# Hybrid encoder step in FP32: the down projection's token operands split piece by piece in the gate/up units, weight tiles kept through both feed-forward stages, the last unit multiplied by quarters

## The chip, the cores and the metric

The kernel runs on one core of one Trainium2 chip. The metric is the device time of one execution in microseconds (us). The kernel before took 2544.37 us, the median of three runs (2538.43, 2544.37 and 2545.0). Engines are called as the profile calls them: PE is TensorE (matmuls), PEld its weight loads, DVE is VectorE, ACT ScalarE, POOL GpSimd, SP SyncE, whose queue issues nearly all DMAs.

## The reference, cut to what matters

One layer of an encoder: attention, an output projection with a residual, then a feed-forward part with a residual, and a last norm. All inputs and outputs are float32. There are 576 new tokens (512 prompt frames and 64 frames of a running stream; 16 meta tokens take part in the attention alone). The change touches only the end:

```python
x = x + mix @ lp['w_out']
h = rmsnorm(x, lp['norm_ffn_g'])
x = x + (jax.nn.silu(h @ lp['ffn_w_gate']) * (h @ lp['ffn_w_up'])) @ lp['ffn_w_down']
...
y_prompt = rmsnorm(xp[:, N_META:], final_norm_g)
y_sample = rmsnorm(xs, final_norm_g)
```

The model width is 2048 and the hidden width of the feed-forward part 5632.

## The kernel before, in words

*Precision.* Every float32 operand of a matmul is split into a high part in the matmul's format (fp32r), written by a copy on ACT, and a low part, the operand less the high part, written by a subtraction on DVE. Three matmuls stand for one: weights high times tokens high, high times low, and low times high. `split` does this for weights, `builder` and `operand` for tokens. Instructions of ACT, DVE and SP go through one wrapper, so that they all have line L125 in the profile; tiles tell them apart: `wh`, `wl` are the weights' parts, `bh`, `bl` the tokens', `ws` sums of weight blocks, `raw` the loaded weights, `m` the PSUM banks, `c` the gate or up result of a unit, `y` the output rows, `ot` the finished output tiles.

*Winograd form.* The three feed-forward matrices are multiplied in a 2 x 2 form with seven products instead of eight (`winograd`, from line 1069). Of the weights, some products take a block as it is loaded (1, 2, 4) and some take a sum of blocks (5, 6, 3, 7): POOL makes two of these sums (line 1096), DVE the other two. Of the tokens there are likewise seven operands: three plain quarters and four sums of quarters. `CHAIN` and `WIDE` give the order of the products and which of them add into the same PSUM bank; `take` moves a bank into the result after each product, and then `step` is called, a hook through which the caller places other work. Matmuls of lines 1127 and 1131 are those of the products (1131 the low weights).

*Gate and up.* The loop over 22 units `u` (line 1281) computes 256 columns of gate, then of up. One product has 8 weight blocks, so 24 matmuls of 128x288; one half of a unit (gate or up) has seven. Weights come in two `raw` blocks of 1 MB for each half, from three buffers (one in the pool `rw`, two in `fr`). After "up", POOL multiplies gate by up in two halves (line 1316) and makes the four sums of quarters for the down projection (1322 to 1325); the result goes to the DRAM tensor `actspill`, the sums to `sumspill`.

*Down projection.* The 22 units are taken in blocks of 4, 4, 4, 4, 4 and 2. For each block a loop over eight pairs of output column tiles (`d`) multiplies the block's weights, by `winograd` with 4 weight blocks (12 matmuls a product), and adds each product into `y`. The operands of the next block are loaded by `builder` from `actspill` and `sumspill` (144 KB each, 28 for a block), and split one step at a time behind the products. There are eight operand slots, four for the current block and four for the next. The operands of block 0 are loaded and split in the last "up" half, from its third product on. The last block of two units is done plainly (`plain_rows`, `mm3` at line 205), token half by token half, and `finish` transposes each half (line 1395), scales it and stores it through `ot`, four buffers in turn.

*Pools.* Tiles live in pools that are opened and closed like a stack. Between the stages `fb` (results and sums of gate/up), `rw` and `fw` (weight parts) are closed, and `yy` (the output rows) and `yp` (weight parts of the down projection) are opened in the same space.

*Order.* PE runs in the order in which a scheduler at build time puts its matmuls; so do the other engines, except for instructions marked by `pin` or by `ordered`, which keep the order of the program text. Each engine then works through its list in order, and so does SP's queue with its DMAs.

Of the kernel before, what the change touches and what calls it, by code (L numbers as in the profile page):

```python
# [2 lines left out]

# [128 lines left out]
def encoder_step(  # L132
# [196 lines left out]
    sumspill = dp.tile([FC // 2, P, 4, QH], F32, name="sumspill")  # L329
    mspill = dp.tile([KC, P, TQ], F32, name="mspill")  # L330
# [674 lines left out]
    rb2 = rw.tile([P, TQ], F32, name="rb2")  # L1005
    sq2 = rw.tile([P, TQ], F32, name="sq2")
# [13 lines left out]

    def operand(m, p, src):
        hi = bc.tile([P, QH], F32R, name=f"bh{p}_{m}")
        lo = bc.tile([P, QH], F32R, name=f"bl{p}_{m}")
        pin(S.activation(hi, src, AF.Copy))
        pin(V.tensor_tensor(lo, src, f32(hi), op=ALU.subtract))
        operands[m, p] = (hi, lo)
# [41 lines left out]

    def winograd(wpool, spool, raws, slots, take, banks=None, engine=V, step=lambda: None, stag=("ws", 3),
# [117 lines left out]
    close_ma()  # L1187
    fb, close_fb = pool("fb", "right")


    def stile():
        return fr.tile([P, QH], F32, name="s", tag="s", bufs=4)

    def combined(c11, c12, c21, c22, chain):
# [15 lines left out]
        def take(p, banks):  # L1210
            if p == 1:
                s[1] = stile()
                S.activation(s[1], banks[1], AF.Copy)
            elif p == 6:
                s[2] = stile()
# [13 lines left out]
    def builder(m0, count, plain, ahead, by_product=False):  # L1229

        srcs = {}
        for m in range(m0, m0 + count):
            quarter = [actspill[2 * m + f, :, c] for f in range(2) for c in (slice(0, QH), slice(QH, TQ))]
            if plain:
                for p, src in zip((1, 2, 4, 5), quarter):
                    srcs[m, p] = src
            else:
                for p, src in zip(ORDER, (quarter[0], quarter[2], sumspill[m, :, 2], sumspill[m, :, 0],
                                          sumspill[m, :, 1], quarter[3], sumspill[m, :, 3])):
                    srcs[m, p] = src  # L1240
        order = [p for p, _ in CHAIN]
        todo = sorted(srcs, key=lambda mp: order.index(mp[1])) if by_product else list(srcs)

        def fetch(n):
            for m, p in todo[n:n + 1]:
                hi = bc.tile([P, QH], F32R, name=f"bh{p}_{m % 8}")
                lo = bc.tile([P, QH], F32R, name=f"bl{p}_{m % 8}")
                load(f32(lo), srcs[m, p])
                operands[m % 8, p] = (hi, lo)

        for n in range(ahead):
            fetch(n)
        for n, (m, p) in enumerate(todo):
            fetch(n + ahead)
            hi, lo = operands[m % 8, p]
            pin(S.activation(hi, f32(lo), AF.Copy))
            yield
            pin(V.tensor_tensor(lo, f32(lo), f32(hi), op=ALU.subtract))
            yield
# [17 lines left out]

    turn = 0
    norm = token_norm()
    start = builder(0, blocks[0], False, 4, True)  # L1280
    for u in range(FC // 2):
        out = {}
        for which, wsrc in (("g", w_gate), ("u", w_up)):
# [9 lines left out]
            take = combined(*quarters(c[:, 0, :], c[:, 1, :]), chain)  # L1293
            done = [0]

            def step():
                if u == 0 and which == "u":
                    next(norm, None)
                if u == FC // 2 - 1 and which == "u":
                    done[0] += 1  # L1300
                    if done[0] > 2:
                        for _ in range(2 * blocks[0]):
                            next(start, None)

            if first:
                winograd(fw, fb, raws, range(4, 8), take, banks0, step=step)
            else:
                winograd(fw, fb, raws, range(8), take, step=step, chain=chain)
# [4 lines left out]
        if u == 0:  # L1313
            gated(g)
        for f in range(2):
            G.tensor_tensor(w[:, f, :], w[:, f, :], g[:, f, :], op=ALU.mult)
            if u < FC // 2 - 1:
                store(actspill[2 * u + f], w[:, f, :])
        if u < FC // 2 - blocks[-1]:
# [6 lines left out]
            store(sumspill[u], t)  # L1326
    for _ in start:
        pass
    for f in range(2):
# [7 lines left out]
    y = []  # L1337

    def plain_rows(m0, n, d, hs, slots, done):
# [3 lines left out]
        for g in range(0, n, 2):  # L1343
            for f in range(2):
                wh = yp.tile([P, 4, P], F32R, name="wh", tag="wh", bufs=2)
                wl = yp.tile([P, 4, P], F32R, name="wl", tag="wl", bufs=2)
# [6 lines left out]
        for f in range(2):  # L1353
            for h in hs:
                c = y[2 * d + f][:, h * QH:(h + 1) * QH]
# [3 lines left out]
    def down_rows(m0, n, d, slots, step):  # L1359
        raws = [load_raw(fr, w_down, m0 * 256, 2 * n, d * 256, 2)]  # L1360
        y11, y12, y21, y22 = quarters(y[2 * d], y[2 * d + 1])
# [6 lines left out]
        winograd(yp, yp, raws, slots, take, step=step, chain=CHAIN)  # L1368
# [3 lines left out]

    def squares(i, h):
        c = y[i][:, h * QH:(h + 1) * QH]
        if i == 0:
            sqs[h] = stile()
            G.tensor_tensor(sqs[h], c, c, op=ALU.mult)
        else:
            t = stile()
# [4 lines left out]
    def finish(h, ahead):  # L1384
# [6 lines left out]
        def turned(q, j):  # L1391
            o, n = tok[h][j]
            ps = pmt()
            for k in range(4):
                PE.transpose(ps[0:n, k * P:(k + 1) * P], y[q * 4 + k][:, o:o + n], ident)
# [7 lines left out]
        vc = yp.tile([P, 3], F32, name=f"vc{h}")  # L1403
        rc = yp.tile([P, 3], F32, name=f"rc{h}")
# [24 lines left out]
    for bi, n in enumerate(blocks):  # L1429
        slots = [(first + k) % 8 for k in range(n)]  # L1430
        if bi + 1 < len(blocks):
            build = builder(first + n, blocks[bi + 1], bi + 2 == len(blocks), 4)
# [4 lines left out]
            for d in range(KC // 2):  # L1437
                if bi == 0:
                    for i in (2 * d, 2 * d + 1):
                        y.append(yy.tile([P, TQ], F32, name=f"y{i}"))  # L1440
                        load(y[i], x2spill[i])
# [3 lines left out]
        else:  # L1445
            before = iter(())
# [10 lines left out]
    close_yp()  # L1457
    close_fr()
    close_yy()
    close_bc()  # L1460
# [74 lines left out]
```

## Time and profile before

| | |
|---|---|
| median of 3 runs | 2544.37 us (2538.43 to 2545.0) |
| the profiled execution, its own time | 2546.21 us |
| its span, first to last instruction | 2544.4 us |
| mean granted TensorE clock | 0.989 |
| PE busy | 2449.5 us, 96% |
| DVE, ACT, POOL busy | 1801.7, 1107.4, 744.8 us |
| gate and up | about 1020 to 1972 us |
| down projection with its end | about 1972 to 2544 us |

The span is the time on which all rows of the trace lie; the execution's own time is 1.8 us longer. Busy shares are averages over stages with different limits, so the stages are looked at one by one. A matmul's busy time is modelled and overlaps the next one's, so the count of matmuls in a stretch says more than the busy share. "A <- B" in a row of waits says that A stood idle until B was done.

### The profile page before, as it was taken

Reading aid. Unit: us, or ns where it says so; the run is one execution under the profiler, and the core shown is the slowest. Engines: PE = TensorE matmul, PEld = TensorE weight load, DVE = VectorE, ACT = ScalarE, POOL = GpSimd, SP = SyncE. Lnnn points to the kernel's source line nnn. Section 1 sums busy time; section 2 is a strip of 40 time slices with the busy share of each in tenths; the row PEclk is TensorE's granted clock in tenths of the full one; section 3 lists DMA queues with packets and bytes.
Section 4 is the critical chain, followed back from the end, with each engine's and each line's share of the span. In section 5 each row is a group of like instructions: output and inputs, shape, how many; then the busy total and the mean of one; then the engine's idle time right before and its main releaser. Section 6 shows DMA issues by size and latency. Waiting matters only on the chain. (4 is left out here: it accounts for less than half of the span.)

```text
span 2544.4 us, 44870 instructions
## 1 busy us (share of the span) xinstructions
PE 2449.5 (96%) x17847; PEld 2390.0 (94%) x17847; DVE 1801.7 (71%) x2826; ACT 1107.4 (44%) x2008; POOL 744.8 (29%) x621
## 2 busy tenths in 40 slices
PE   7999999989999999999999999999999899999997
PEld 6999999988999888999999999999999899999997
DVE  5555555556555567877777777777777899999975
ACT  5343333334434344444444444444445444444445
POOL 0000000010000165644545445454543222222236
PEclk9999999999999999999999999999999999999999
DMA  6533232334232453333333333333335642542334
GB/s 197 156 87 87 80 85 75 82 94 143 88 92 80 152 154 117 123 133 119 124 101 130 124 123 133 115 119 108 128 128 162 210 150 83 164 150 83 114 97 149
DMA packets 330116, 307.73 MB, mean 121 GB/s; under 512 B 24708, under 2 KB 298507, under 8 KB 329907
## 3 DMA queue, kind: packets, MB, share of 16 engines
q1 hardware_dynamic: 329346, 302.80, 37.9%
q8 instruction: 140, 2.29, 0.4%
q0 software_dynamic: 560, 2.06, 0.2%
q14 instruction: 70, 0.57, 0.1%
HBM read 250.82 MB, written 56.68 MB: 121 GB/s over the span
## 5 line engine op out<-in xcount | busy, mean ns | idle before, releaser
L1127 PE MATMUL m<-bh,wh 128*128 128x288 f32 x3584 | 968.9, 296 | 10.8 <-ACT wh L125 10.7
L1127 PE MATMUL m<-bl,wh 128*128 128x288 f32 x3584 | 968.1, 295 | 0.0
L1127 PEld LDWEIGHTS m<-bh,wh 128*128 128x128 f32 x3584 | 674.5, 188 | 11.8 <-ACT wh L125 11.7
L1127 PEld LDWEIGHTS m<-bl,wh 128*128 128x128 f32 x3584 | 678.0, 189 | 0.1
L1131 PE MATMUL m<-bh,wl 128*128 128x288 f32 x3584 | 585.9, 299 | 18.4 <-DVE wl L125 15.4
L1131 PEld LDWEIGHTS m<-bh,wl 128*128 128x128 f32 x3584 | 512.8, 189 | 31.9 <-DVE wl L125 31.4
L1096 POOL TENSOR_TENSOR ws<-raw 128x512 f32<-128x512 f32 x256 | 344.0, 1352 | 600.5 <-DVE wl L125 321.7
L125 ACT ACTIVATE wh<-ws 128x512 fp32r<-128x512 f32 (+1 forms) x340 | 288.8, 849 | 449.4 <-PE m L1127 300.8
L125 DVE TENSOR_TENSOR wl<-ws,wh 128x512 fp32r<-128x512 f32 (+1 forms) x340 | 379.5, 1116 | 115.1 <-ACT wh L125 114.5
L125 DVE TENSOR_TENSOR wl<-raw,wh 128x512 fp32r<-128x512 f32 x416 | 403.5, 984 | 25.9 <-ACT wh L125 16.1
L125 ACT ACTIVATE wh<-raw 128x512 fp32r<-128x512 f32 x416 | 249.8, 626 | 310.3 <-PE m L1127 277.3
L108 PE MATMUL ps<-xh,wh 128*128 128x296 f32 x960 | 222.1, 313 | 4.9 <-ACT xh L125 3.7
L108 PE MATMUL ps<-xl,wh 128*128 128x296 f32 x960 | 212.0, 302 | 0.8 <-DVE xl L125 0.8
L108 PE MATMUL ps<-xh,wl 128*128 128x296 f32 x960 | 211.9, 302 | 0.9 <-DVE wl L125 0.9
L108 PEld LDWEIGHTS ps<-xh,wh 128*128 128x128 f32 x960 | 157.8, 192 | 9.0 <-ACT xh L125 3.8
L125 DVE TENSOR_TENSOR y<-y,m 128x288 f32<-128x288 f32 x312 | 140.0, 449 | 28.7 <-PE m L1131 17.9
L108 PEld LDWEIGHTS ps<-xh,wl 128*128 128x128 f32 x960 | 158.3, 191 | 1.6 <-DVE wl L125 1.6
L108 PEld LDWEIGHTS ps<-xl,wh 128*128 128x128 f32 x960 | 158.7, 192 | 1.1 <-DVE xl L125 1.1
L125 DVE TENSOR_TENSOR ws<-ws,raw 128x512 f32<-128x512 f32 x128 | 92.4, 722 | 84.3 <-POOL ws L1096 77.6
L125 DVE TENSOR_TENSOR wl<-wr,wh 128x1024 fp32r<-128x1024 f32 (+1 forms) x110 | 119.6, 1087 | 44.5 <-ACT wh L125 43.0
L125 ACT ACTIVATE wh<-wr 128x1024 fp32r<-128x1024 f32 (+1 forms) x110 | 101.7, 929 | 73.1 <-PE ps L108 51.7
L1274 POOL TENSOR_TENSOR c<-c,rb 128x576 f32<-128x576 f32 x44 | 73.2, 1666 | 165.5 <-ACT c L125 162.9
(359 smaller groups left out, 3352.7 us busy)
## 6 DMA issues: line engine op xcount, KB each, us to landing
raw<-in_ffn_w_gate SPq DMA_DIRECT2D x44, 1024.0 KB, 7.2
raw<-in_ffn_w_up SPq DMA_DIRECT2D x44, 1024.0 KB, 5.9
raw<-in_ffn_w_down SPq DMA_DIRECT2D x40, 1024.0 KB, 5.7
wr<-in_w_in SPq DMA_DIRECT2D x60, 512.0 KB, 4.0
actspill<-c SPq DMA_DIRECT2D x44, 288.0 KB, 2.1
sumspill<-c SPq DMA_DIRECT2D x20, 576.0 KB, 2.8
bl<-sumspill SPq DMA_DIRECT2D x80, 144.0 KB, 3.6
bl<-actspill SPq DMA_DIRECT2D x68, 144.0 KB, 3.9
```

The source lines that it names most:

```text
L108: self.tc.keep_in_program_order(self.pe.matmul(out, lhsT, rhs, start=start, stop=stop))
L125: ins = issue(*args, **kwargs)
L1096: engine.tensor_tensor(w[:, k:k + m, :], pick(xs), pick(ys), op=op)
L1127: PE.matmul(banks[p], wh[:, k, :], x, start=first and new and k == 0 and x is hi, stop=False, skip_group_check=not new)
L1131: PE.matmul(banks[p], wl[:, k, :], hi, start=False, stop=last and k == n - 1, skip_group_check=not new)
L1274: G.tensor_tensor(g[:, f, :], g[:, f, :], rb2, op=ALU.mult)
```

## The change

1. **Token operands split in the gate/up loop.** Units 2 to 19 no longer store their result and sums for the down projection as they are. In the next unit, `parts` splits the seven operands one at a time (ACT high part, DVE low part, into a tile of two parts) and stores each with both parts in a new DRAM tensor `partspill`. In the down projection `fetcher` loads the two parts (288 KB) straight into the operand slot. Units 0 and 1 keep the old way, and so do the last two units, which the plain block uses.
2. **Block 0.** `starter` loads its operands after each product of the last "up" half, from the first product on, and splits only those of units 0 and 1, two products later. SP's order is pinned there. The weights for its first two column pairs are fetched ahead by `fetch_raw`, the first before that half, the second after it.
3. **Weight tiles.** `fw` (weight parts) and a new pool `fs` (sums of weight blocks) stay open through both stages. `weight_tiles` gives the down projection, which needs tiles of four blocks, the two halves of a tile of eight.
4. **Output rows.** `y0` and `y1` take the space of the two norm rows, `y2` to `y4` that of the weight buffer in `rw`; the others come from `yy`, which is opened after the first column pair.
5. **Last unit.** Its multiplication of gate by up is done in quarters on POOL, each when its quarter is complete.
6. **Last block.** Sums of squares and output tiles lie in free operand slots (30 of them) instead of tiles of four buffers.

The number and shapes of the matmuls are the same. The diff, cut to its core:

```diff
+    def weight_tiles(wpool, n):
+        if n == 8 or not spare:
+            both = [wpool.tile([P, 8, P], F32R, name=x, tag=x, bufs=2) for x in ("wh", "wl")]
+            if n == 8:
+                return both
+            spare.append([w[:, 4:8, :] for w in both])
+            return [w[:, 0:4, :] for w in both]
+        return spare.pop()
...
-            wh = wpool.tile([P, n, P], F32R, name="wh", tag="wh", bufs=2)
-            wl = wpool.tile([P, n, P], F32R, name="wl", tag="wl", bufs=2)
+            wh, wl = weight_tiles(wpool, n)
...
+    def fetch_parts(m, p):
+        load(f32(operand_tile(m % 8, p)), partspill[m, :, PIECE[p]])
...
+    def starter():
...
+        todo = [p for p, _ in CHAIN]
+        for i in range(len(todo) + 2):
+            if i < len(todo):
+                for m in range(blocks[0]):
+                    if m < WHOLE:
+                        fetch_whole(m, todo[i], whole(m, todo[i]))
+                    else:
+                        fetch_parts(m, todo[i])
+            if i > 1:
+                for m in range(WHOLE):
+                    split_in_place(m, todo[i - 2])
+            yield
...
+    def parts(u, srcs):
+        for p in ORDER:
+            b = fb.tile([P, 2, QH], F32R, name="parts", tag="parts", bufs=2)
+            S.activation(b[:, 0, :], srcs[PIECE[p]], AF.Copy)
+            V.tensor_tensor(b[:, 1, :], srcs[PIECE[p]], f32(b[:, 0, :]), op=ALU.subtract)
+            store(partspill[u, :, PIECE[p]], f32(b))
+            yield
...
+            ending = u == FC // 2 - 1 and which == "u"
+            if ending:
+                Q.ordered = True
+                fetch_raw(0, blocks[0], 0)
...
+                def take(p, banks):
+                    combine(p, banks)
+                    if p in (2, 7, 3, 4):
+                        q = {2: 0, 3: 1, 4: 2, 7: 3}[p]
+                        G.tensor_tensor(w[q], w[q], g[q], op=ALU.mult)
...
+                done[0] += 1
+                if which == "u" or done[0] > 3:
+                    next(pieces, None)
+                if ending:
+                    next(start)
...
+            if u < WHOLE:
+                store(sumspill[u], t)
+            else:
+                pieces = parts(u, [b11, b12, b21, b22] + [t[:, i, :] for i in range(4)])
     for _ in start:
         pass
+    fetch_raw(0, blocks[0], 1)
...
+    accumulator(0, rw.tile([P, TQ], F32, name="y0", tag="rows", bufs=2))
+    accumulator(1, rw.tile([P, TQ], F32, name="y1", tag="rows", bufs=2))
+    y234 = rw.tile([P, 8 * 256], F32, name="y234", tag="raw", bufs=1)
...
-    close_fb()
-    close_rw()
-    yy, close_yy = pool("yy", "right")
-    close_fw()
-    yp, close_yp = pool("yp")
...
-            build = builder(first + n, blocks[bi + 1], bi + 2 == len(blocks), 4)
+            if bi + 2 == len(blocks):
+                build = builder(first + n, blocks[bi + 1], 4)
+            else:
+                build = fetcher(first + n, blocks[bi + 1])
...
-            ot = yp.tile([P, 512], F32, name="ot", tag="ot", bufs=OT_BUFS)
+            ot = room(others)[:, 0:512]
```

More of the change, by code (lines that the diff above doesn't have):

```diff
@@ L1 @@
+import itertools
 import math
@@ L1298, in step @@
                     next(norm, None)
[L1299 to L1303, printed above, removed]
+                done[0] += 1
[3 more added lines that the diff above has]
+                    next(start)
             if first:
-                winograd(fw, fb, raws, range(4, 8), take, banks0, step=step)
+                winograd(fw, fs, raws, range(4, 8), take, banks0, step=step)
             else:
-                winograd(fw, fb, raws, range(8), take, step=step, chain=chain)
+                winograd(fw, fs, raws, range(8), take, step=step, chain=chain)
             out[which] = c
@@ L1314, in encoder_step @@
             gated(g)
+        for _ in pieces:
+            pass
+        if u == FC // 2 - 1:
+            break
         for f in range(2):
             G.tensor_tensor(w[:, f, :], w[:, f, :], g[:, f, :], op=ALU.mult)
-            if u < FC // 2 - 1:
+            if u < WHOLE or FC // 2 - blocks[-1] <= u < FC // 2 - 1:
                 store(actspill[2 * u + f], w[:, f, :])
@@ L1445, in encoder_step @@
         else:
+            rest = [m for m in range(8) if m not in slots]
+            sums = itertools.cycle([f"b{p}_{rest[-1]}" for p in ORDER])
+            others = iter([f"b{p}_{m}" for m in rest[-2::-1] for p in ORDER])
             before = iter(())
```

135 lines of the change are left out of this document (82 added, 53 removed).

## The prediction

> **What bounds the kernel now.** I read the page's busy shares first, then the busy times by stretch (columns: stretch, its length, busy us and count of PE, PEld, DVE, ACT, POOL, the granted clock, DMA share, GB/s).
>
> ```profile
> span 2544.4 us, 44870 instructions
> PE 2449.5 (96%) x17847; PEld 2390.0 (94%) x17847; DVE 1801.7 (71%) x2826; ACT 1107.4 (44%) x2008; POOL 744.8 (29%) x621
> core 0: us, PE busy (x) PEld busy (x) DVE busy (x) ACT busy (x) POOL busy (x), PEclk, DMA share, GB/s
> 1145.00:1908.00 763.00, 763.00 (x5737) 763.00 (x5736) 570.47 (x651) 334.48 (x514) 378.01 (x273) 1.00 0.36 121
> 1972.00:1990.00 18.00, 9.03 (x45) 8.44 (x45) 11.63 (x20) 6.38 (x15) 6.87 (x5) 0.72 0.96 324
> 1990.00:2395.00 405.00, 390.81 (x2848) 379.26 (x2847) 375.60 (x661) 189.58 (x356) 89.14 (x67) 1.00 0.42 131
> 2395.00:2461.00 66.00, 65.13 (x487) 64.43 (x486) 56.23 (x93) 25.29 (x40) 12.94 (x10) 1.00 0.27 81
> ```
>
> TensorE bounds it. A busy share of matmuls hides small stalls, so I count matmuls instead. Gate and up (1145 to 1908) make 5737 in 763 us: 0.133 us each, with PE never idle. That is the floor. In the down projection 2848 matmuls need 378.8 us and take 405: 26.2 us lost. In its last 66 us 487 need 64.8: 1.2 lost. At the stage change (1972 to 1990) 45 need 6.0 and take 18: 12.0 lost. These 39 us, and the tail, are all that the change can win without fewer matmuls, and it has as many.
>
> What ends PE's waits (from 1990 to 2461 and at the stage change), and what VectorE does meanwhile (1990 to 2395; count, busy us, mean ns):
>
> ```profile
> PE m L1131 <- DVE wl L125: 12.1, 23, 1.0
> L125 DVE TENSOR_TENSOR y<-y,m 128x288 f32<-128x288 f32 x238 | 106.7, 448 | 10.1 <-PE m L1131 8.9
> L125 DVE TENSOR_TENSOR wl<-ws,wh 128x512 fp32r<-128x512 f32 x136 | 101.4, 746 | 0.0
> L125 DVE TENSOR_TENSOR bl<-bl,bh 128x288 fp32r<-128x288 f32 x118 | 78.3, 664 | 0.0
> PE m L1127 <- ACT wh L125: 8.1, 1, 8.1
> 1973.78 1.86 SPq L125 DMA_DIRECT2D actspill<-c  x2
> 1980.19 0.63 ACT L125 ACTIVATE wh<-raw 128x512 fp32r<-128x512 f32 x1 [1.15 <-DMA actspill<-c]
> ```
>
> In the down projection VectorE is busy 375.6 of 405 us; every PE wait there is for the low part of a weight split, and 78.3 us of VectorE's time are the token splits (bl); the accumulations (y) and weight splits (wl) stay. The stretch after 2395, where those are over, loses 1.8% instead of 6.5%. At the stage change the first weight split stands behind the store of the last unit (issued at 1973.8), since the new pool takes the space of the old ones, and PE waits 8.1 us.
>
> **The change part by part.** I call the end of the last gate/up matmul T0 (1972.6 in before).
>
> *Token splits leave the down projection.* 118 x 0.664 = 78.3 us leave VectorE in the 405 us (375.6 falls to 297, 73%). The weight tiles of four units become halves of tiles of eight: a split may start when the pair before last is multiplied, so it has about one product (12 x 0.133 = 1.6 us) more of lead. Bounds: nothing more than the stretch after 2395 shows, 26.2 - 405 x 1.8% = 18.8 us gained; or all 27.4. Since two things are removed at once and that stretch had only one of them, I take 24.
>
> *They go into the next gate/up unit.* Units 2 to 19 each get 7 ACT copies, 7 VectorE subtractions and 7 stores of 288 KB, in place of one sum store and two of act. One unit is 2 x 7 x 24 x 0.133 = 44.7 us. Cover:
>
> ```profile
> 1950.00:1972.00 22.00, 22.00 (x168) 22.00 (x167) 20.90 (x39) 16.85 (x36) 3.67 (x2) 1.00 0.86 250
> 1526.66 1.82 POOL L1316 TENSOR_TENSOR c<-c 128x576 f32<-128x576 f32 x1 [0.45 <-DVE c L125]
> 1526.49 4.96 DVE L125 TENSOR_TENSOR wl<-raw,wh 128x512 fp32r<-128x512 f32 x4
> 1530.87 1.25 POOL L1324 TENSOR_TENSOR c<-c 128x288 f32<-128x288 f32 x1
> 1531.12 1.06 ACT L125 ACTIVATE wh<-ws 128x1024 fp32r<-128x1024 f32 x1 [1.76 <-PE m L1127]
> 1546.98 0.69 DVE L125 TENSOR_TENSOR wl<-raw,wh 128x512 fp32r<-128x512 f32 x1
> 1535.20 0.38 SPq L125 DMA_DIRECT2D raw<-in_ffn_w_up  x1
> 1540.39 1.51 POOL L1096 TENSOR_TENSOR ws<-raw 128x512 f32<-128x512 f32 x1 [1.51 <-DMA raw<-in_ffn_w_up]
> L125 ACT ACTIVATE c<-m 128x288 f32<-128x288 f32 x136 | 55.9, 411 | 0.7
> L125 ACT ACTIVATE bh<-bl x148: 425/429/447, 1955.1 to 2388.8; 128x288 fp32r<-128x288 f32 x148
> ```
>
> Before's last half unit (1950 to 1972) carries 28 such splits with 168 matmuls in 22 us: no loss, at 95% of VectorE. But POOL is nearly idle there. In a normal unit ACT and VectorE keep order, and the third piece is the sum that POOL finishes last (1530.87 + 1.25 = 1532.1). Behind it on ACT stand a copy, a piece and the weights of the fourth product. Those are split at 1531.12 now, when the second product's high pass is over; they are needed 8 x 0.133 + 24 x 0.133 later, near 1535.2. After the change: 1532.1 + 0.4 (VectorE's first new subtraction stands ahead of the accumulation that POOL's second multiplication, at 1526.66, waits for) + 0.43 + 0.41 + 0.43 + 1.06 = 1534.8. The margin is 0.4 us, each unit. The second weight block of "up" (1535.20) also moves behind five stores, some 1.5 us later, and POOL waits for that load already (1540.39). A VectorE subtraction beside POOL's sums can take 1.24 us (4.96 / 4) instead of 0.45, 0.8 more. So the cost is 0 to 0.8 us in each of 18 units, 0 to 14 in all. I take 0.3: 5 us lost.
>
> The Trainium skill, "SBUF — State Buffer", section "SBUF: two separate sides", says that a VectorE instruction with two SBUF inputs and a GpSimd one take a port pair in turn, each blocked for the whole of the other. That speaks against this change, which puts two such subtractions beside POOL's sums. The trace agrees: a split took 1.24 us there and 0.69 with POOL idle (1546.98).
>
> *The stage change.* Weight pools stay open, block 0's first weights are loaded one half unit early, and its operands are split from the first product on. So the 8.1 us wait goes, and PE runs straight on. What is late next: in the changed program's order VectorE's first accumulation into y stands behind a weight sum of the second column pair, and that load stands on SP's queue behind the last operand loads, which wait for T0.
>
> ```profile
> raw<-in_ffn_w_down SPq DMA_DIRECT2D x38, 1024.0 KB, 5.6
> 1980.33 2.52 POOL L1096 TENSOR_TENSOR ws<-raw 128x512 f32<-128x512 f32 x2 [5.04 <-DMA bl<-sumspill]
> L125 DVE TENSOR_TENSOR ws<-ws,raw 128x512 f32<-128x512 f32 x34 | 23.6, 693 | 18.3 <-POOL ws L1096 16.2
> 1980.87 0.61 PE L1127 MATMUL m<-bh,wh 128*128 128x288 f32 x1 [8.09 <-ACT wh L125]
> 1988.22 0.29 PE L1127 MATMUL m<-bl,wh 128*128 128x288 f32 x1
> ```
>
> Load out at T0 + 0.3, landed 5.6 later or up to 2.7 more (the four operand loads ahead, 0.88 MB at the 324 GB/s of 1972 to 1990): T0 + 7.2 taken. Then POOL 1.26, VectorE 0.69 and the accumulation 0.45: T0 + 9.6. PE has products 1, 5 and 2 first, 3 x 1.6 = 4.8; product 6 reuses the bank. Stall 4.8 us. In before the wait was followed by 7.3 us (1980.87 to 1988.2) of slow issue, 3.9 us beyond the wait itself; I take 2.7 for a stall half as long. The load for the third pair follows 20 y and operand loads (5.6 MB, 17 us at 324 GB/s), lands near T0 + 7.2 + 17 + 5.6 = 30. PE wants it after 14 products (22.3) and 7.5 of stall, also near T0 + 30, and POOL's and VectorE's sums come between: about 2 more. Sum 9.5 against 12.0: 2.5 gained. Ends: 12 gained if that load is early, 3 lost if both are late.
>
> A wait of 1.44 us later in the trace was also followed by half-rate matmuls (0.44 us instead of 0.29):
>
> ```profile
> 2505.27 0.41 PE L205 MATMUL m<-bh,wh 128*128 128x288 f32 x1 [1.44 <-ACT wh L125]
> 2507.34 0.44 PE L205 MATMUL m<-bl,wh 128*128 128x288 f32 x1
> 2506.37 0.30 PE L205 MATMUL m<-bl,wh 128*128 128x288 f32 x1
> ```
>
> The Trainium skill, "TensorE: Matmul & The Clock Gate", section "What's actually happening", says that the clock halves after an idle window of about 3.4 us. By that rule a stall cut below it would cost no slow issue, 2.7 us less; these rows, slow after 1.44 us, speak against counting on it.
>
> *Last block and tail.* The half tiles give plain_rows the same lead, and the output tiles come from 24 free operand slots instead of 4 in turn.
>
> ```profile
> PE m L205 <- DVE wl L125: 2.4, 7, 0.4
> PE m L205 <- ACT wh L125: 1.9, 2, 1.4
> ACT ot L125 <- DMA out<-ot: 4.3, 4, 2.3
> 2532.00:2544.00 12.00, 3.38 (x16) 2.62 (x16) 4.87 (x9) 4.54 (x8) 0.00 (x0) 0.74 0.56 197
> ```
>
> Of 4.3 us waiting in the last block I take 3 (0 to 6, with what follows each wait). At the end 12 us at 197 GB/s, 2.4 MB, leave; at 324 GB/s that is 7.3 us, so of the 4.3 us in which ACT waits for earlier stores I take 2 (0 to 4).
>
> *Quarters and the rest.* The last unit's multiplication by quarters (POOL) ends sooner, but nothing but its two stores waits for it: 0. The extra reads, 28 x 288 KB per block against 28 x 144, raise 131 GB/s by about 45, under the 324 seen: 0.
>
> **Sum:** 24 - 5 + 2.5 + 3 + 2 = 26.5. The profiled execution took 2546.2 us (span 2544.4 and 1.8 around it): 2519.7. The runs' median, 2544.4, is 1.8 lower, so 2518.
>
> **The rivals.** (a) *Gate/up stays unharmed and the stalls all go:* 27.4 + 6 + 2.5 + 5 = 41 us, about 2503. For it: the full half unit at 1950. Against: POOL idle there. (b) *The stall in gate/up is 0.8 us a unit:* 14 instead of 5, and the steady gain only 18.8: 2532. For it: the 0.4 us margin and the 4.96 us row. (c) *Slower:* the wait for POOL's last sum on ACT decides. If wh comes over 1.75 us late in each of 18 units, the 31.5 us of gains (24 + 2.5 + 3 + 2) are used up. With both subtractions blocked ahead of the accumulations, POOL's chain comes 2 x 1.24 + 0.45 later, 2.5 us over the margin: 18 x 2.5 = 45, 2558. For it: everything behind ACT's wait keeps order. Against: from 1145 to 1908 VectorE was idle 25% and ACT 56% of the time. (d) *The change doesn't do what it says:* stage change no better, because the stall on the second load replaces the one removed: 2.5 less and 3 lost, 2524; in the range anyway.
>
> **How the numbers follow.** Forecast with (d), 2508 to 2527: 0.52. (a): 0.17. (b): 0.17. (c): 0.11. A remainder near no change (loads of gate/up late by a microsecond a unit): 0.03. Range: from (a) less 3 to (b) plus 10, 2500 to 2542, leaving out (c) and half of the remainder. A measurement here tells 0.3% (7.6 us) from no change: faster 0.85, same 0.04, slower 0.11.
>
> **What would show it.** In the changed profile: down blocks at 0.133 to 0.134 us per matmul with VectorE near 75%; no PE wait over 1 us there; at T0 no gap, then one of 3 to 6 us after three products, VectorE waiting for POOL's ws and that for the w_down load; gate/up still 5700 matmuls in about 763 us (770 would be my 0.3 us a unit or more); no ot waiting for out. Wrong would be: ACT waiting for POOL's sums and PE for wh in every unit, or VectorE still over 85% in the down blocks.

## The result: 0.64% slower

The changed kernel takes 2558.73 us (median of 4 runs, 2557.24 to 2561.46) against 2543.84 for the kernel before; the ratio is 1.0064 (95% interval 1.0049 to 1.0079). Forecast were 2518 us, with a chance of 0.11 for the rival that came true. The profiled execution took 2558.11 us, span 2556.3, so the two traces differ by 11.9 us.

The top of the changed kernel's page, and its busy times by stretch (columns as in the prediction; the first stretch is the same 763 us of gate and up, the next two are the first block of the down projection, then come blocks 1 to 4, then the last block and the tail):

```profile
span 2556.3 us, 44980 instructions
PE 2449.0 (96%) x17847; PEld 2388.6 (93%) x17847; DVE 1839.6 (72%) x2826; ACT 1078.3 (42%) x2008; POOL 778.5 (30%) x623
```

```profile
core 0: us, PE busy (x) PEld busy (x) DVE busy (x) ACT busy (x) POOL busy (x), PEclk, DMA share, GB/s
1145.00:1908.00 763.00, 740.18 (x5473) 730.25 (x5472) 641.80 (x732) 349.88 (x604) 385.72 (x261) 1.00 0.40 133
2007.00:2025.00 18.00, 9.88 (x58) 9.64 (x58) 10.32 (x17) 5.08 (x11) 3.81 (x4) 0.72 0.99 341
2025.00:2110.00 85.00, 82.76 (x620) 82.22 (x620) 67.28 (x117) 29.46 (x51) 19.99 (x14) 1.00 0.66 222
2110.00:2469.00 359.00, 358.24 (x2690) 357.07 (x2689) 294.70 (x519) 131.99 (x233) 91.91 (x62) 1.00 0.49 160
2469.00:2556.00 87.00, 69.37 (x493) 64.15 (x491) 50.78 (x88) 44.57 (x82) 49.15 (x62) 0.93 0.44 139
```

Count matmuls again. In 763 us of gate and up there are now 5473 instead of 5737: 264 matmuls, 35 us, are missing, with VectorE at 84%. In blocks 1 to 4, 2690 matmuls take 359 us, 0.1335 each: the down projection runs at the floor, with VectorE at 82% instead of 93%. So the gain is there, and it is paid for where TensorE had never waited. Below, a "piece" is one of a unit's seven token operands, split and stored in the next unit; "halves" are the halves of a weight tile of eight blocks.

From the start times of the matmuls in each trace I get the stages to 0.1 us; all runs below are read in the same way. "Block 0" counts from the last gate/up matmul. The stages are those of one profiled execution; the medians of the experiments come from three chips, on which the kernel before had medians of 2543.4 to 2544.4.

| us | gate and up | block 0 | blocks 1 to 4, each | last product to end | median of runs |
|---|---|---|---|---|---|
| before | 991.8 | 106.6 | 95.2 | 84.7 | 2543.8 |
| changed | 1028.5 | 102.6 | 89.8 | 87.5 | 2558.7 |
| e1_order | 1005.4 | 104.0 | 89.9 | 88.1 | 2541.4 |
| e2_spread | 991.5 | 103.2 | 89.8 | 87.4 | 2526.7 |
| e3_nopieces | 991.7 | 104.2 | 91.4 | 88.0 | 2532.0 |
| e4_ends | 1028.3 | 105.1 | 89.9 | 83.6 | 2558.2 |
| e5_whole_tiles | 1001.3 | 107.6 | 91.6 | 83.0 | 2532.8 |
| e6_spread_plain | 991.5 | 104.8 | 89.8 | 83.8 | 2521.6 |
| e7_turn | 991.5 | 93.4 | 90.1 | 83.6 | 2510.8 |
| e8_three | 991.5 | 95.1 | 89.9 | 84.0 | 2512.6 |
| e9_order3 | 1017.3 | 102.2 | 89.9 | 88.1 | 2548.9 |

The change by stages: 36.7 lost in gate and up, 4.0 gained in block 0, 21.6 (4 x 5.4) in blocks 1 to 4, 2.9 lost at the end, and 2.2 gained ahead of the first of these matmuls, where the runs differ by 3.4 among themselves. Sum 11.8 lost, of 11.9.

**Where TensorE waits in gate and up.** The waits of the changed kernel from 1070 to 1985 (engine and line, what it waited for: us in all, times, longest), those with the pieces and those of TensorE:

```profile
ACT parts L125 <- POOL c L1393: 112.2, 36, 5.1
...
ACT parts L125 <- DMA partspill<-parts: 64.3, 38, 3.8
...
ACT parts L125 <- POOL c L1401: 34.8, 18, 1.9
...
PE m L1144 <- ACT wh L125: 12.2, 17, 1.5
PE m L1144 <- ACT c L125: 9.9, 14, 2.1
...
PE m L1148 <- DVE wl L125: 1.7, 4, 0.7
```

ACT waits for POOL's products and last sum, and for the stores of earlier pieces, and TensorE waits for what stands behind on ACT. One unit's beginning shows the chain (timeline of the changed kernel, by engine: start, busy us, instruction, and in brackets the idle time before it and what ended it; the half unit's first matmul starts at 1211.88):

```profile
1210.68 2.51 DVE L125 TENSOR_TENSOR wl<-raw,wh 128x512 fp32r<-128x512 f32 x2
1213.16 1.02 DVE L125 TENSOR_TENSOR parts<-c,parts 128x288 fp32r<-128x288 f32 x1
1214.10 0.81 DVE L125 TENSOR_TENSOR c<-c,m 128x288 f32<-128x288 f32 x2
...
1214.99 1.81 POOL L1393 TENSOR_TENSOR c<-c 128x576 f32<-128x576 f32 x1 [1.12 <-DVE c L125]
...
1218.98 1.25 POOL L1401 TENSOR_TENSOR c<-c 128x288 f32<-128x288 f32 x1
...
1220.27 0.45 ACT L125 ACTIVATE parts<-c 128x288 fp32r<-128x288 f32 x1 [1.95 <-POOL c L1401]
1220.62 0.39 ACT L125 ACTIVATE c<-m 128x288 f32<-128x288 f32 x1
1220.91 0.44 ACT L125 ACTIVATE parts<-c 128x288 fp32r<-128x288 f32 x1
1221.24 1.05 ACT L125 ACTIVATE wh<-ws 128x1024 fp32r<-128x1024 f32 x1
...
1227.71 0.45 ACT L125 ACTIVATE parts<-c 128x288 fp32r<-128x288 f32 x1 [2.29 <-DMA partspill<-parts]
1228.06 1.04 ACT L125 ACTIVATE wh<-ws 128x1024 fp32r<-128x1024 f32 x1
```

Read it from the top. A piece's subtraction (1.02 us beside POOL) stands ahead of the accumulations; so POOL's second multiplication starts 3.1 us after the half unit's first matmul, 1.1 in the row of before that the prediction quotes (there the half unit starts at 1525.56). POOL's last sum ends at 1220.23. ACT stands 1.95 us for it with the third piece, and only then come the copy, another piece and the weights of the fourth product, ready at 1222.29; the fourth product should start at 1221.47 and starts at 1222.34. Six us later ACT stands 2.29 us for the store of the piece two before (two tiles for the pieces), and the sixth product is late by 0.6. Ahead of the gate halves' fourth and sixth products TensorE stands 13.4 and 12.7 us over the stage (time between starts less 0.133 us each). The other 10 or so of the 36.7 us lie at other places and in matmuls that start late by less.

**At the stage change** (the last gate/up matmul, T0, ends at 2007.2; timeline of SP, POOL, DVE and PE in the changed kernel):

```profile
2008.69 0.76 SPq L125 DMA_DIRECT2D raw<-in_ffn_w_down  x1
...
2031.09 0.38 SPq L125 DMA_DIRECT2D raw<-in_ffn_w_down  x1
...
2016.84 2.48 POOL L1113 TENSOR_TENSOR ws<-raw 128x512 f32<-128x512 f32 x2 [6.85 <-DMA raw<-in_ffn_w_down]
...
2018.13 1.73 DVE L125 TENSOR_TENSOR ws<-ws,raw 128x512 f32<-128x512 f32 x1 [5.10 <-POOL ws L1113]
...
2020.29 2.29 PE L1144 MATMUL m<-b,wh 128*128 128x288 f32 x8 [8.12 <-DVE y L125]
```

This is the chain that the prediction drew (load, POOL, VectorE, accumulation), with a stall of 8.1 us by this row (8.3 from start to start, less 0.133) instead of 4.8; the load at 2031.09 is that of the third pair, which costs another 1.9 and 0.6.

**In the last block** ACT's timeline has a period of its own:

```profile
2476.39 0.54 ACT L125 ACTIVATE y<-y,gT 128x288 f32<-128x288 f32 x1 [2.33 <-POOL b L1469]
2476.83 1.14 ACT L125 ACTIVATE wh<-raw 128x512 fp32r<-128x512 f32 x2
...
2480.78 0.54 ACT L125 ACTIVATE y<-y,gT 128x288 f32<-128x288 f32 x1 [2.34 <-POOL b L1469]
2481.22 1.14 ACT L125 ACTIVATE wh<-raw 128x512 fp32r<-128x512 f32 x2
```

The two weight splits of a column pair, one right after the other, come behind a scaling of y that waits for POOL's squares, every 4.39 us, while the 24 matmuls of a column pair need 3.2.

### The profile page after: what moved, and what is told of

Same layout as the page of the kernel before. It is cut to its first block, busy times and chain, and to the rows that moved or that the text cites. A ratio compares the mean times of both kernels' runs of the same rounds, so it can differ in the third digit from the quotient of the medians.

```text
span 2556.3 us, 44980 instructions
## 1 busy us (share of the span) xinstructions
PE 2449.0 (96%) x17847; PEld 2388.6 (93%) x17847; DVE 1839.6 (72%) x2826; ACT 1078.3 (42%) x2008; POOL 778.5 (30%) x623
## 3 DMA queue, kind: packets, MB, share of 16 engines
q8 instruction: 140, 2.29, 0.4%
## 5 line engine op out<-in xcount | busy, mean ns | idle before, releaser
L1144 PE MATMUL m<-b,wh 128*128 128x288 f32 x7168 | 1053.9, 296 | 34.3 <-ACT wh L125 15.0
L1144 PEld LDWEIGHTS m<-b,wh 128*128 128x128 f32 x7168 | 985.4, 189 | 44.6 <-ACT wh L125 20.7
L1148 PE MATMUL m<-b,wl 128*128 128x288 f32 x3584 | 583.2, 298 | 5.1 <-DVE wl L125 4.9
L1113 POOL TENSOR_TENSOR ws<-raw 128x512 f32<-128x512 f32 x256 | 389.2, 1531 | 569.5 <-DVE wl L125 280.6
L1148 PEld LDWEIGHTS m<-b,wl 128*128 128x128 f32 x3584 | 514.6, 189 | 9.5 <-DVE wl L125 8.5
L125 DVE TENSOR_TENSOR wl<-raw,wh 128x512 fp32r<-128x512 f32 x416 | 393.9, 970 | 25.8 <-ACT wh L125 25.2
L125 ACT ACTIVATE wh<-raw 128x512 fp32r<-128x512 f32 x416 | 242.8, 621 | 223.8 <-PE m L1144 205.8
L125 DVE TENSOR_TENSOR ws<-ws,raw 128x512 f32<-128x512 f32 x128 | 114.3, 895 | 99.0 <-POOL ws L1113 96.5
L125 ACT ACTIVATE parts<-c 128x288 fp32r<-128x288 f32 x126 | 55.6, 442 | 211.3 <-POOL c L1393 112.2
L125 DVE TENSOR_TENSOR parts<-c,parts 128x288 fp32r<-128x288 f32 x126 | 103.6, 823 | 23.6 <-ACT parts L125 23.6
```

Source lines behind the costliest of these rows:

```text
L125: ins = issue(*args, **kwargs)
L1113: engine.tensor_tensor(w[:, k:k + m, :], pick(xs), pick(ys), op=op)
L1144: PE.matmul(banks[p], wh[:, k, :], x, start=first and new and k == 0 and x is hi, stop=False, skip_group_check=not new)
L1148: PE.matmul(banks[p], wl[:, k, :], hi, start=False, stop=last and k == n - 1, skip_group_check=not new)
```

## The experiments

The planner that sets each engine's list puts an instruction where it takes its inputs to be ready, not where the code has it; in the changed kernel's list for ACT, a piece follows the weights of each of the gate half's first three products, and all seven stand ahead of the weights of its last two, where the code has the first after the fourth product. Theory A, *place*: the pieces are pulled forward to a unit's beginning, and there they wait, ahead of weights on ACT's list, for POOL's last sum and for stores. Theory B, *amount*: 126 more subtractions on VectorE, slow beside POOL. Theory C, *queue*: weight loads behind five stores on SP.

**e1_order**

```diff
-        for p in ORDER:
+        for p in (1, 2, 3, 5, 6, 7, 4):
```

> The seven pieces of a unit go in the order 1, 2, 3, 5, 6, 7, 4, so that the sum which POOL finishes last comes seventh instead of third; nothing else differs from the changed kernel. Its 18 units with pieces average 46.75 us against 44.71 without; of the 2.04 lost, some 0.85 is a stall ahead of the fourth product of the gate half and some 0.7 one ahead of the sixth. Theory A (place): ACT, in order, stands behind POOL's last sum, and later behind the store of a piece two before, and the weights' copy stands behind ACT. Then the first of the two stalls goes and the second stays: gate and up 1028.5 -> about 1013, the whole 2558 -> 2543. Theory B (amount): 126 more VectorE subtractions, 0.82 us each beside POOL's sums, delay everything wherever they stand: 1028 stays within 3 us. Theory C (the second weight block's load stands behind five stores on SP's queue): 1028 stays as well, and the stall follows POOL's wait for raw.

Measured: 2541.39 us (ratio to before 0.9992, 0.9983 to 1.0001: no different from before), gate and up 1005.4. The new order, in which operands 3 and 7 change places too, wins 23 us, more than A gave it, and not as A had it: the stalls ahead of the fourth product only halve (13.4 to 5.9 us), and those ahead of the sixth are gone. B and C fall as the main cause, since nothing but the order has changed. POOL's wait for the weights of "up", which C goes by, does not follow the loss either: 33.7 us before, 52.0 changed, 34.8 here (13.7 us still lost), 35.5 in e2_spread (nothing lost), 24.6 in e9_order3 (25.5 lost).

**e2_spread**: an instruction held behind the one traced before it on its engine can't be pulled forward.

```diff
-                S.activation(copied[p], banks[p], AF.Copy)
+                tc.keep_in_program_order(S.activation(copied[p], banks[p], AF.Copy))
...
-            S.activation(b[:, 0, :], srcs[PIECE[p]], AF.Copy)
-            V.tensor_tensor(b[:, 1, :], srcs[PIECE[p]], f32(b[:, 0, :]), op=ALU.subtract)
+            tc.keep_in_program_order(S.activation(b[:, 0, :], srcs[PIECE[p]], AF.Copy))
+            tc.keep_in_program_order(
+                V.tensor_tensor(b[:, 1, :], srcs[PIECE[p]], f32(b[:, 0, :]), op=ALU.subtract))
```

(and the accumulations of `take_sums` on VectorE in the same way)

> The same seven pieces, each held on ACT and on VectorE behind the instruction traced before it on that engine, so that they come one a product from the gate half's fourth product to the up half's third, as the code is written, instead of being pulled forward in a bunch at the unit's start. As much work as in the changed kernel, at other places. Theory A (place): no piece waits for POOL or for a store, gate and up fall from 1028.5 to 992 to 998 us, the whole to 2522 to 2528. Theory B (amount): with as many subtractions and as many of POOL's sums, gate and up stay above 1015. Theory C (queue): in between, since the stores are then spread over 22 us and the weight loads no longer stand behind five of them; POOL's wait for raw (52 us in all) would fall with it.

Measured: 2526.71 us (0.9944, 0.9925 to 0.9964), gate and up 991.5 in the profiled execution (2525.04 us): no loss at all there. Two of the ten runs took 2541 and 2543 us, and neither of them left a profile. By stretch, and the places that answer to those of the changed kernel (half unit from 1213.51):

```profile
1145.00:1908.00 763.00, 763.00 (x5737) 763.00 (x5736) 633.33 (x771) 374.46 (x634) 402.39 (x273) 1.00 0.41 141
```

```profile
1214.81 1.82 POOL L1394 TENSOR_TENSOR c<-c 128x576 f32<-128x576 f32 x1
...
1226.80 0.44 ACT L125 ACTIVATE parts<-c 128x288 fp32r<-128x288 f32 x1
...
1229.99 0.44 ACT L125 ACTIVATE parts<-c 128x288 fp32r<-128x288 f32 x1
```

5737 matmuls, as before the change, with all pieces in. POOL's second multiplication is back at 1.3 us after the first matmul, and the first piece comes 13 us after it, when POOL's sums are long done. Place, not amount: theory A. Pieces still wait for stores (51.9 us in all), now with room behind them.

**e3_nopieces**

```diff
-    WHOLE = 2
+    WHOLE = FC // 2 - 2
...
-                build = fetcher(first + n, blocks[bi + 1])
+                build = builder(first + n, blocks[bi + 1], 4, False)
```

(`builder` loads each operand whole, from `actspill` or `sumspill`, and splits it in place; `starter` the same for all of block 0)

> No pieces: the units' tokens are stored whole as in the kernel before and split in the down projection, one every second step; all else of the change stays (half tiles, open pools, quarters, output tiles). It parts what leaves the down projection with the splits from what the half tiles give. Gate and up: 992 to 994 us, as before the change, whatever theory. Down projection's blocks 1 to 4, 95.2 us each before and 89.8 changed (89.4 at 0.133 us a matmul): if the splits on VectorE were the cause of the stalls, they stay at 93 to 96; if the half tiles' lead alone hides the low part of the weights, they are at 90 to 91, and the pieces cost 36 us for nothing. Whole: 2540 to 2545 by the first, 2520 to 2526 by the second.

Measured: 2532.01 us (0.9959, 0.9945 to 0.9973); blocks 1 to 4 at 91.4. That is nearer to the second answer: without the pieces, the halves, with whatever else of the change acts in these blocks, win 15.0 (4 x 3.76) of the 21.6 us, and VectorE is nearly as full as before (91%):

```profile
2075.00:2440.00 365.00, 361.27 (x2686) 357.18 (x2685) 331.59 (x604) 159.29 (x315) 88.93 (x62) 1.00 0.40 124
```

**e5_whole_tiles**, the other half of it: e2_spread without the halves.

```diff
-        if n == 8 or not spare:
-            both = [wpool.tile([P, 8, P], F32R, name=x, tag=x, bufs=2) for x in ("wh", "wl")]
...
+        both = [wpool.tile([P, 8, P], F32R, name=x, tag=x, bufs=2) for x in ("wh", "wl")]
+        return [w[:, 0:n, :] for w in both]
```

> The spread pieces of the run before, and the weight tiles of four units no longer halves of a tile of eight: each pair has tiles of its own, two in turn, as before the change. It is the fourth corner beside before (neither), the run without pieces (halves alone, blocks 1 to 4 at 91.4 us each) and the spread pieces (both, 89.8). Gate and up stay at 991 to 992. If the token splits on VectorE are what makes the low parts of the weights late, blocks 1 to 4 are at 90 to 91 without the halves too; if the halves' lead does, they are at 93 to 95. Last block: 83.6 us from the last product to the end, as in the run with tiles of its own there, against 87.4. Whole: 2524 to 2527 by the first, 2536 to 2543 by the second.

Measured: 2532.80 us (0.9952, 0.9938 to 0.9967); blocks 1 to 4 at 91.6, so without the token splits alone 14.4 us are won. My either-or was wrong: each alone brings two thirds, both together the whole, and the second of them adds some 7 us. Against 89.4 at 0.133 us a matmul, either alone leaves a loss of some 2%, neither 6%, both under 0.5%. The profiled execution took 2540.15 us, 7 above the median; its gate and up lost 10 us from unit 16 on, where ACT stood for a store ahead of weights (next instruction: `wh`):

```profile
1724.66 0.45 ACT L125 ACTIVATE parts<-c 128x288 fp32r<-128x288 f32 x1 [4.57 <-DMA partspill<-parts]
```

**e4_ends**

```diff
-                s = sums[2] = subtotal(n, engine, ALU.subtract, [sums[1]], a11)
+                with tc.issue_after(behind[-1]) if behind else contextlib.nullcontext():
+                    s = sums[2] = subtotal(n, engine, ALU.subtract, [sums[1]], a11)
...
-                wh, wl = weight_tiles(fw, 4)
+                wh, wl = (w[:, 0:4, :] for w in weight_tiles(fw, 8))
```

(`behind[-1]` is the accumulation of the fifth product of the pair before, in block 0; the second edit is in `plain_rows`)

> The changed kernel with two edits at places that lie far apart and are read apart by their windows. One: in the first block of the down projection VectorE's weight sum of the next column pair is held behind the accumulation of the fifth product of the pair before, so that VectorE no longer waits for the second pair's load ahead of the first accumulations. Now PE stands 8.3 us after three products, then 1.9 and 0.6; if VectorE's order is the cause, 2 us or less are left and the first block falls from 102.6 to 93 to 96 us; if the late load itself is, PE stands as long one pair later and the block stays above 100. Two: the last block splits its weights into tiles of their own, two in turn, as before the change. From the last product of the five blocks to the end 87.5 us now, 84.7 before; if the halves, split two at once, are the cause, 84 to 85; if the operand slots or the accumulators' new places are, 87 stays. Together 2546 to 2549 us, against 2558.

Measured: 2558.19 us (1.0062, 1.0047 to 1.0077). The last block is as expected, 83.6 instead of 87.5: the halves cost 3.9 us there. The first edit missed: in block 0 TensorE stands 5.9, 3.4 and 1.9 us instead of 8.3, 1.9 and 0.6, and block 0 takes 105.1. The timeline of VectorE, SP's queue and POOL in block 0, and of ACT in the last block:

```profile
2018.01 1.01 DVE L125 TENSOR_TENSOR y<-y,m 128x288 f32<-128x288 f32 x2 [4.24 <-DMA y<-x2spill]
...
2021.89 7.77 SPq L125 DMA_DIRECT2D y<-x2spill  x12
...
2032.36 0.38 SPq L125 DMA_DIRECT2D raw<-in_ffn_w_down  x1
...
2040.77 2.52 POOL L1114 TENSOR_TENSOR ws<-raw 128x512 f32<-128x512 f32 x2 [20.89 <-DMA raw<-in_ffn_w_down]
...
2486.34 0.62 ACT L125 ACTIVATE wh<-raw 128x512 fp32r<-128x512 f32 x1
...
2490.20 0.61 ACT L125 ACTIVATE wh<-raw 128x512 fp32r<-128x512 f32 x1
```

VectorE no longer waits for POOL, but for the accumulator y itself, still loading; and the third pair's weights are issued behind twelve accumulators, and TensorE stands 3.4 us there. So VectorE's order is not enough; the loads are late as well. The last two rows, each the first of a column pair's two splits, lie 3.86 us apart instead of 4.39.

**e6_spread_plain**: the edits of e2_spread and the second one of e4_ends.

> Spread pieces, and whole tiles in the last block alone: 2526.7 less the 3.8 us that the last block lost, 2522 to 2524. Rival: the two are not independent, since the last block now begins with other tiles in flight: 2526.

Measured: 2521.63 us (0.9925, 0.9902 to 0.9948): 5.1 less than e2_spread. At the end the profiled execution gains 3.6 (87.4 to 83.8), as the same edit did in e4_ends (3.9), so the two are independent there; the rest of the 5.1 is less than the runs scatter (2517 to 2546 here).

**e7_turn**: e6_spread_plain, the first edit of e4_ends, and SP's list in order of need through block 0.

```diff
+            if i == 1:
+                for k in range(2):
+                    accumulator(k, rw.tile([P, TQ], F32, name=f"y{k}", tag="rows", bufs=2))
+            if i == len(todo) - 1:
+                fetch_raw(0, blocks[0], 1)
...
-                    Q.ordered = False
...
+                    fetch_raw(first, n, 2)
...
+                if bi == 0 and d:
+                    for i in (2 * d + 4, 2 * d + 5):
+                        if i < KC:
+                            accumulator(i, yy.tile([P, TQ], F32, name=f"y{i}"))
+                    if d == KC // 2 - 1:
+                        Q.ordered = False
+                    elif (first, d + 1) not in fetched:
+                        fetch_raw(first, n, d + 1)
```

> As the run with spread pieces and whole tiles in the last block, and the loads at the stage change in the order of need on SP's list: the first two accumulators in the last half unit, the second pair's weights ahead of the last product's operands, each further pair's weights one pair ahead, the other accumulators two a pair and the next block's operands between them, instead of twelve accumulators and eight operands ahead of the third pair's weights. VectorE's sum for the next pair is held behind the fifth product's accumulation, as in the run on the ends. The first block takes 103.2 us, 89.4 at 0.133 us a matmul. Theory D (order of the loads): the stalls of some 8 and 3 us go, the block falls to 91 to 96, the whole to 2510 to 2516. Theory E (sum of the loads: 318 to 383 GB/s from 2000 to 2050 at full engines): whatever the order, what PE needs by then comes as late; the block stays above 99 and the whole above 2518.

Measured: 2510.79 us (0.9876, 0.9861 to 0.9891), block 0 at 93.4: theory D. Stretch, queue and the two waits that are left:

```profile
1970.00:1988.00 18.00, 14.58 (x109) 14.17 (x108) 16.16 (x27) 7.67 (x15) 5.14 (x4) 1.00 1.03 364
```

```profile
1968.47 0.38 SPq L125 DMA_DIRECT2D raw<-in_ffn_w_down  x1
...
1981.43 0.38 SPq L125 DMA_DIRECT2D raw<-in_ffn_w_down  x1
...
1975.73 1.29 PE L1146 MATMUL m<-b,wh 128*128 128x288 f32 x8 [1.98 <-DVE y L125]
...
1980.59 1.29 PE L1146 MATMUL m<-b,wh 128*128 128x288 f32 x8 [1.44 <-DVE y L125]
```

The second pair's weights go out 1.9 us ahead of the last gate/up matmul (1970.4) instead of 1.5 behind it, the third's at 11 instead of 24 us after it. The DMA engines are as full as before (364 against 341 GB/s), so it was the order and not the sum. VectorE's sum is held as well in this run; e4_ends has that hold without the new order (block 0 at 105.1), and the new order without the hold was not run. At 1.2% below the kernel before, this kernel and e8_three, which can't be told from it, are the fastest here.

**e8_three**: e7_turn, with a third tile for the pieces (the row of the sum of squares, no longer needed then).

```diff
+            if next(third):
                 b = fb.tile([P, 2, QH], F32R, name="parts", tag="parts", bufs=2)
+            else:
+                b = rw.tile([P, TQ], F32R, name="parts", tag="row0", bufs=1)
...
```

> As the run with spread pieces, whole tiles in the last block and the loads in the order of need (2510.8; single times from 2508 to 2520), and every third piece in the tile that held the sum of squares, so that a piece waits for the store of the piece three before it instead of two. The spread runs scatter more than before (2522 to 2543 and 2517 to 2546), and the one whose profile shows it has ACT waiting 4.6 and 5.8 us for the store of a piece, ahead of a weights' copy. If that wait makes the scatter, single times now lie within 5 us of each other, and the median falls to 2506 to 2510. If it does not, both stay.

Measured: 2512.64 us (0.9872, 0.9855 to 0.9889), 4 runs from 2507.9 to 2513.6; e7_turn's 4 lay between 2508.4 and 2520.1. The median didn't fall. The scatter looks smaller, but four runs against four don't show it; what makes it stays open.

**e9_order3**: e1_order with the same third tile.

> As the run with POOL's last sum as the seventh piece (gate and up 1005.4 us, 13.7 above the 991.7 of before), with a third tile for the pieces in the same way. If what is left there is the wait for the store of the piece two before, the second half of theory A, gate and up fall to 992 to 996 and the whole from 2541 to 2528 to 2532. If the bunched subtractions themselves are what is left, 1003 to 1006 and 2539 to 2542 stay.

Measured: 2548.94 us (1.0021, 1.0012 to 1.0031), gate and up 1017.3: 12 us worse, where I had expected 10 better. In its order on ACT two pieces now stand ahead of the weights of the fourth and of the fifth product where one stood in e1_order. It seems that the free tile let the planner pull them further forward; that is a reading of one unit and is not shown. It fits A. The "second half" of A was not tested by this run: ACT's waits for stores became fewer (15 for 31) but not shorter in all (33.3 for 33.9 us), so what makes up e1_order's last 13.7 us stays open, but for what e2_spread shows: that a later place removes them.

## Why the prediction was wrong

- **Down projection, 24 us taken: right.** Blocks 1 to 4 gained 21.6, and block 0 behind the stage change some 5 more (it lost 17.2 us against the floor of 89.4 before, 12.0 of them at the stage change itself). What I had not seen is that either of the two removals brings some 15 alone, so the pieces were worth some 7 us here. The lower bound of 18.8, read off a stretch without splits, was too high for that removal alone: e5_whole_tiles has 14.4.
- **Gate and up, 0.3 us a unit taken, 0 to 0.8 as bounds: this step failed.** It was 2.04, 36.7 us in all instead of 5. The chain was the right one: third piece, POOL's last sum, weights of the fourth product, margin 0.4 us. I let POOL come 0.4 us later, for one subtraction of 0.4; it came 1.8 later (last sum 8.35 us after the half unit's first matmul instead of 6.56), for the subtraction takes 1.02 there and the chain begins later (POOL's first multiplication 1.0 us ahead of that matmul instead of 2.05). And I followed that one wait only: the wait for the store of the piece two before was in none of the terms. Rival (c) priced the same place at 2.5 us a unit and 2558; that is the measured time, but by chance: its cost of 45 us was 36.7, of which the place that it priced has 13.4 and the one behind that other wait 12.7, and its gains of 31.5 were 22.7. The argument against (c), VectorE idle 25% and ACT 56%, was no argument: e2_spread has as much work and no loss. Idle shares say that there is room somewhere, not that there is room ahead of the instruction that TensorE needs next.
- The prediction had the planner's order on ACT before it (behind the third piece a copy, a piece and the weights of the fourth product), but it did not ask what e2_spread asks: whether the pieces cost anything at a later place.
- **Port.** The Trainium skill, "SBUF — State Buffer", section "SBUF: two separate sides", says that a VectorE instruction with two SBUF inputs and a GpSimd one exclude each other. The traces agree: a piece's subtraction takes 0.82 us on the mean in the changed kernel (103.6 for 126) and 0.67 in e2_spread (84.7), and in the unit shown above 1.02 us while POOL works and 0.46 at 1220.74, when POOL stands idle. But e2_spread shows that this alone does not cost TensorE time.
- **Stage change, 2.5 us gain taken: wrong.** Counted in matmuls, 10.3 us are lost in the 18 us from 2007 and 2.5 up to 2110, 12.8 against 12.0 before, so about 1 was lost. The stall was 8.3 and not 4.8, and 1.9 and 0.6 for the third pair (2 forecast). The named chain was right, its terms were too small: the load went out 1.5 us after T0 instead of 0.3, took 8.2 to POOL's start instead of 6.9, and VectorE's sum took 1.73 beside POOL instead of 0.69. That the order on SP's queue is the remedy, together with the hold of VectorE's sum, only e7_turn shows.
- **Last block and tail, 5 us taken, 0 as the lower bound: wrong in sign.** 2.9 were lost. With the halves, whose lead helps the blocks, ACT makes both weight splits of a column pair in a row behind a scaling that waits for POOL, 4.39 us a column pair; with tiles of its own it is 3.86 (e4_ends). Without the halves the rest of that edit gains about 1 us (84.7 to 83.8 in e6_spread_plain).
- **Quarters, reads: 0.** No wait in the changed kernel's trace ends with a load of parts, so in the blocks this was right. On SP's queue, though, eight such loads stand ahead of the third pair's weights in block 0, where e7_turn wins.
- **Rival (a)** adds 6 and 5 us without a name; the bounds given are 6 for the last block and 4 for the tail. It changes nothing here.

## What to carry over

Work moved into a stage whose bound engine never waits is not paid by busy shares: ask which in-order list it joins, what it waits for there, and what the bound engine needs from behind it. If a planner places it by readiness, pin it late, behind work that needs nothing from it, and compare the order before a trace is read. When two edits remove one stall, try each alone: the cheap one may carry most of it.

## What the runs showed of the hardware

- After the 8.1 us wait at the stage change, some 20 matmuls started 0.24 us apart instead of 0.133, and the granted clock of those 4 us is 0.50; after the waits of 2.0 and 1.4 us in e7_turn the very next spacing but one is 0.133 again, and the clock 1.00:

```profile
2020.00:2024.00 4.00, 3.71 (x15) 3.72 (x16) 1.48 (x5) 1.15 (x2) 0.00 (x0) 0.50 1.04 402
```

```profile
1975.00:1979.00 4.00, 3.27 (x24) 3.21 (x24) 3.65 (x7) 1.25 (x3) 2.27 (x2) 1.00 1.05 400
```

The first row is of the changed kernel, the second of e7_turn. But short waits were followed by half the clock too. In the kernel before, behind the wait of 1.44 us whose rows the prediction shows, the clock is 0.50 from 2507 to 2510 (first row below). In the changed kernel one wait of 2.05 us in gate and up has 0.57 in the 4 us behind it (next two rows):

```profile
2507.00:2510.00 3.00, 3.00 (x15) 3.00 (x14) 2.20 (x4) 1.10 (x2) 1.33 (x2) 0.50 0.69 209
...
1745.18 3.91 PE L1144 MATMUL m<-b,wh 128*128 128x288 f32 x16 [2.05 <-ACT c L125]
...
1745.00:1749.00 4.00, 3.82 (x17) 3.82 (x18) 3.91 (x4) 1.37 (x3) 1.27 (x1) 0.57 0.97 310
```

In e4_ends, the other way round, a wait of 3.25 us was followed by 8 matmuls at a clock of 0.99 (2041.4 to 2043.2). The Trainium skill, "TensorE: Matmul & The Clock Gate", section "What's actually happening", has the clock halved after an idle window of about 3.4 us. The wait of 8.1 us and those of e7_turn fit that, the waits of 1.44 and 2.05 us do not, so the prediction was right not to count on it. Here the length of a wait does not tell by itself whether the clock falls; what does stays open.

- The runs with spread pieces scatter more than the kernel before: e2_spread 2522 to 2543 and e6_spread_plain 2517 to 2546 at the same granted clock, the kernel before 2538 to 2549 in all its runs. The profiled execution of e5_whole_tiles shows one way to such a loss, ACT standing 4.57 us for the store of a piece; whether that makes the scatter stays open.
